# Mixture of experts on one core: weights split 2048 columns at a time, tokens gathered and outputs added by indirect DMA

## The chip, the cores and the metric

One core of one Trainium2 chip. The metric is the device time of one execution in microseconds (us), the median of three runs. Engines: PE (TensorE) multiplies matrices, DVE (VectorE) and ACT (ScalarE) work elementwise, POOL (GpSimd) and SP (SyncE) issue DMAs here.

## The reference, cut to what matters

The reference runs two blocks of two layers each on 256 tokens of 1024 features. The second layer of the second block has a mixture of experts in place of a feed-forward layer, and the change is there:

```python
def moe_swiglu(x2d, w_router, w_gate, w_up, w_down):
    ...
    top_logits, top_e = lax.top_k(logits, TOP_K)
    top_w = jax.nn.softmax(top_logits, axis=-1).reshape(-1)
    ...
    def expert_block(args):
        xb, e = args
        return (jax.nn.silu(xb @ w_gate[e]) * (xb @ w_up[e])) @ w_down[e]
    ...
    y = jax.ops.segment_sum(y_rows[dest] * w_sorted[:, None], tok_sorted, num_segments=n_tok)
```

There are 8 experts with an inner width of 3584, each token goes to two of them, and all is float32.

## The kernel before

Every product is made from float32 operands that are split into two parts of the type fp32r: a high half `h`, which ACT casts (line 368), and a low half `l`, which DVE makes as value minus `h` (line 369). `mm3` (lines 381 to 385) then adds three matmuls into one PSUM bank: high by high, high by low, low by high.

`moe` (line 1976) computes the norm `u` of the tokens, the router's logits and, for each token and expert, a weight, whether it is chosen, and its place among the expert's tokens. An expert has 128 places. Then it goes through the experts in order, and `expert` (line 2115) does the work of one.

- *Gather.* `gather` (line 2098) builds `D`, 0 or 1 for token by place, on DVE (line 2103), and multiplies `u` by it on PE (line 2111): 16 matmuls in float32 that give the expert's tokens, features on partitions. ACT and DVE split them to `xh` and `xl`. The gather of the next expert is called by `ahead()` in `expert`, after the last gate and up block.
- *Weights.* An expert's weights are 42 pieces of 128 x 2048, 1 MiB each: for each of 14 column blocks `ck`, two pieces for gate and up and one for down. `arrive` (line 349) fetches them by SP's queue into a ring of `NM` = 8 tiles `wv`. `parts` (line 358) splits 1024 columns at a time into tiles `wh` and `wl`; they come in turn from two rings of three pairs, so six pairs are there.
- *A block.* `up(ck)` multiplies the tokens by both gate and up pieces (24 matmuls of 512 columns into one bank); between the two it calls `turned(ck - 1)`, which transposes the block before (line 2129) and splits it to `me_hh` and `me_hl`. After it ACT takes the silu (line 2156) and DVE multiplies (line 2157). `down(ck - 1)` then adds 12 matmuls into the two banks `y`.
- *Back to the tokens.* At its end (lines 2169 to 2189) an expert transposes `D`, puts the weights in order of places (line 2173), scales and splits `y` to `me_yh` and `me_yl`, multiplies by the turned `D` (8 matmuls of 512 columns, lines 2187 and 2188), and DVE adds the result to the tokens `x` (four additions, line 2189).

After the eight experts a loop handles experts with more than 128 tokens; it runs as often as there are such experts.

The kernel is written as a sequence; the framework orders the instructions of each engine when the program is built, each as soon as its estimate has operands and a buffer ready, earlier ones first. On the chip each engine keeps that order, and semaphores hold it where an operand is not there. So PE may take matmuls of the next expert between those that end the last one, as the rows below show.

Of the kernel before, what the change touches and what calls it, by code (L numbers as in the profile page):

```python
# [11 lines left out]
F32 = mybir.dt.float32  # L12
F32R = mybir.dt.float32r
BF16 = mybir.dt.bfloat16
I32 = mybir.dt.int32
# [6 lines left out]
PIECE = 2048  # L22
# [67 lines left out]
def constants():  # L90
    t = Table()
    i = np.arange(128)
    r, c = i[:, None], i[None, :]
    t.add("ident", (r == c) * 1.0)
    t.add("causal", np.where(c > r, NEG, 0.0))
    d = i % 64
    t.add("freq", np.where(d < 8, -FREQ[d % 8], np.where(d < 16, FREQ[d % 8], 0.0)))
    d = i % 32
    t.add("freq_i", np.where(d < 4, -FREQ_I[d % 4], np.where(d < 8, FREQ_I[d % 4], 0.0)))
    t.add("freq_2", np.broadcast_to(FREQ_2, (128, 16)))  # L100

# [24 lines left out]
    t.add("eye64", (e == x[:, None]) * 1.0)  # L126
    t.add("g_strict", np.where(e < x[:, None], 0.0, NEG))
    t.add("g_incl", np.where(e >= x[:, None], 0.0, NEG))
    t.add("first", np.broadcast_to(np.where(np.arange(256) % 64 == 0, 0.0, 1.0), (128, 256)))
    t.add("before", (r < c) * 1.0)  # L130
    t.add("slot", np.broadcast_to(c, (128, 128)) * 1.0)
    f = np.arange(8)
    t.add("lower_e", np.broadcast_to((f[None, :] < f[:, None]) * 1.0, (128, 8, 8)))
    return t
# [118 lines left out]
ROUND = 12582912.0  # L253
NV, NH, NL = 3, 3, 3
NM = 8
PRE = ['31111111111111111', '11311131101111113']
COUNTS = ['111111121222211223022', '111111121322211222120']
ORDER = ['gmggmggmgmgmgmgggmggmggmggmggmggm', 'gmgggmgmgmgmggmgmgmggggmggmggmggm']
# [2 lines left out]
class Core:  # L261
# [96 lines left out]
    def parts(self, v, ring=None):  # L358
        n = v.shape[1]
        pool, _, nh, nl = ring or next(self.rings)  # L360
        h = pool.tile([128, HALF], F32R, tag="wh", name=self.name("wh"), bufs=nh)[:, :n]
        l = pool.tile([128, HALF], F32R, tag="wl", name=self.name("wl"), bufs=nl)[:, :n]
        self.split(h, l, v)
        return h, l

    def split(self, h, l, v):

# [1594 lines left out]
    def moe_first(self, pool):  # L1962

        rt = self.load(pool, "router", [128, 64])
        rh, rl = (self.sb(pool, [128, 8, 8], F32R) for _ in range(2))
        self.split(rh, rl, rt.rearrange("p (k e) -> p k e", k=8))
        return rh, rl, {n: self.cst(pool, n) for n in ("before", "slot", "lower_e")}

    def moe_ahead(self, ctx):

        self.big_ring(ctx, NM, 3, 3, side="right")
        self.moe_gain = self.row(self.arriving[0], "norm_ffn1")
        for j in (0, 1, 3, 4, 2, 6, 7, 5)[:NM]:
            self.early.append(self.arrive(self.A["moe"][j], True))

    def moe(self, rh, rl, c):
        nc, A = self.nc, self.A
        mm = nc.tensor.matmul
        with ExitStack() as ctx:
            pool = self.pool(ctx, "moe")  # L1980
            self.banks(mm=4, acc=4)

            x = self.feature_major(self.x, self.vec("norm_ffn1"))
# [1 line left out]
            p = self.psum()[:8, :256]  # L1985
            for k in range(8):
                self.mm3(p, (rh[:, k], rl[:, k]), (x[0][:, k], x[1][:, k]), k == 0, k == 7)
            lT = self.sb(pool, [8, 256])
            nc.vector.tensor_copy(lT, p)
            rc = self.norm_col(pool, z)  # L1990
            for n in range(4):
                for tt in range(2):
                    h = slice(n * 256, n * 256 + 256)
                    nc.scalar.activation(u[:, tt, h], self.x[:, tt, h], AF.Copy, scale=rc[tt])
                    nc.gpsimd.tensor_mul(u[:, tt, h], u[:, tt, h], self.moe_gain[:, h])
            ones = self.sb(pool, [128, 128])
            nc.gpsimd.memset(ones, 1.0)
            lg = self.sb(pool, [128, 2, 8])
            p = self.psum()[:, :16].rearrange("p (t e) -> p t e", t=2)
            for tt in range(2):  # L2000
# [77 lines left out]
            self.halves = itertools.cycle((0, 1))  # L2078
            chosen = lambda e: [[info[:, tt, j, e:e + 1] for j in range(3)] for tt in range(2)]
            ready = self.gather(pool, c, u, chosen(0))  # L2080
            for e in range(8):

                following = []
                ahead = (lambda: following.append(self.gather(pool, c, u, chosen(e + 1)))) if e < 7 else lambda: None
                self.expert(pool, ready, lambda i: moe[e, i], ahead, None if e else rest)
                ready = following[0] if following else None

            n = nc.values_load(count, min_val=0, max_val=3)
            with self.tc.For_i(0, n) as s:  # L2089
                lt = self.sb(pool, [128, 8], F32, "lt")  # L2090
                nc.sync.dma_start(lt, spill[bass.ds(s, 1)].rearrange("s p e -> (s p) e"))
                le = self.sb(pool, [1, 1], I32, "le")
                nc.vector.tensor_copy(le, lt[:1, 6:7])
                e = nc.sync.value_load(le, min_val=0, max_val=7)
                ready = self.gather(pool, c, u, [[lt[:, 3 * tt + j:3 * tt + j + 1] for j in range(3)] for tt in range(2)])
                self.expert(pool, ready, lambda i: moe[bass.ds(e, 1), i].rearrange("e p c -> (e p) c"), lambda: None)

    def gather(self, pool, c, u, info):

        nc = self.nc  # L2100
        D = self.sb(pool, [128, 2, 128], F32, "me_D", 2)
        for tt in range(2):
            last = nc.vector.tensor_scalar(D[:, tt], c["slot"], info[tt][2], info[tt][1], op0=ALU.is_equal, op1=ALU.mult)
# [11 lines left out]
    def expert(self, pool, ready, w, ahead, first=None):  # L2115


        nc = self.nc
# [14 lines left out]
            hs[ck] = hh, hl  # L2133

        def down(ck):
            d = self.arrive(w(3 * ck + 2))
            d = [self.parts(d[:, j * HALF:j * HALF + HALF]) for j in range(2)]
            hh, hl = hs.pop(ck)
            for j in range(2):
                for n in range(2):  # L2140
                    s = slice(n * 512, n * 512 + 512)
                    self.mm3(y[n], (hh[:, j], hl[:, j]), [t[:, s] for t in d[j]], ck == 0 and j == 0, ck == 13 and j == 1)

        def up(ck):
            p = self.psum()
            for i in range(2):
                v = self.arrive(w(3 * ck + i))
                for j in range(2):
                    h, l = [t.rearrange("p (k c) -> p k c", k=2) for t in self.parts(v[:, j * HALF:j * HALF + HALF])]
                    for k in range(2):  # L2150
                        kk = 4 * i + 2 * j + k
                        self.mm3(p, (xh[:, kk], xl[:, kk]), (h[:, k], l[:, k]), kk == 0, kk == 7)
                if i == 0 and ck:
                    turned(ck - 1)
# [4 lines left out]
        for ck in range(14):  # L2159
# [3 lines left out]
                first()  # L2163
            if ck:
                down(ck - 1)
        turned(13)
        ahead()
        down(13)
        p = self.psum()[:, :384]
        for tt in range(2):  # L2170
            nc.tensor.transpose(p[:, tt * 128:tt * 128 + 128], D[:, tt], self.ident)
        for tt in range(2):
            mm(p[:, 256:257], D[:, tt], weight[tt], start=tt == 0, stop=tt == 1)
        Dt = self.sb(pool, [128, 256], F32R, "me_Dt", 1)
        nc.scalar.copy(Dt, p[:, :256])
        wr = self.sb(pool, [128, 1], F32, "me_w", 2)
        nc.vector.tensor_copy(wr, p[:, 256:257])
        yh = self.sb(pool, [128, 1024], F32R, "me_yh", 1)
        yl = self.sb(pool, [128, 1024], F32R, "me_yl", 1)
# [60 lines left out]
```

## Time and profile before

| | |
|---|---|
| median of three runs | 3272.34 us (3271.23 to 3272.56) |
| the profiled execution, its own time | 3261.19 us |
| its span, first to last instruction | 3259.4 us |
| busy, share of the span | PE 96%, DVE 74%, ACT 57%, POOL 1% |
| experts, about | 2195 to 3220 us of the span |
| DMA, whole span | 691.10 MB, mean 212 GB/s |

PE is the matmul, PEld its weight load, which overlaps. Times in rows are in us from the span's start unless they are marked ns. A row of a timeline merges several like instructions (x4) and gives the time from the first's start to the last's end; in brackets stands how long the engine had been idle and what released it. Ends of matmuls are modelled (a matmul of 512 columns shows 0.39 us and the next one starts 0.23 later), so the starts tell the pace. A float32 matmul shows as two records; a transpose shows as one.

### The profile page before, as it was taken

How to read it: one execution, taken by the hardware profiler on the slowest of the kernel's cores; microseconds unless marked ns; L12 is line 12 of the kernel's file. 1: busy time of each engine (PE TensorE's matmuls, PEld its weight loads, DVE VectorE, ACT ScalarE, POOL GpSimd, SP SyncE). 2: the span in 40 equal slices, each digit the busy share in tenths (PEclk: the TensorE clock that was granted, in tenths of full speed). 3: DMA queues.
4: the chain of work that ended last, by engine and by line, in shares of the span. 5: the costliest groups of instructions: out<-in, count | busy, mean ns of one | idle time of the engine just before them, and what ended most of it. 6: DMA issues, size and time to landing. Idle time of an engine off the chain costs nothing. (4 is left out here: it accounts for less than half of the span.)

```text
span 3259.4 us, 52984 instructions
## 1 busy us (share of the span) xinstructions
PE 3135.3 (96%) x20906; PEld 2712.3 (83%) x20906; DVE 2399.8 (74%) x4079; ACT 1846.6 (57%) x2810; POOL 45.1 (1%) x87
## 2 busy tenths in 40 slices
PE   8998999999999899999998999989999999999998
PEld 8987699999779888888997888878887777777876
DVE  6567765656865686866557858569888888888886
ACT  5455544444454455544445445448777777777775
POOL 0000000000000000000001000000000000000000
PEclk9998999999999999999999999999999999999999
DMA  8434373551365143337733423479999898898994
GB/s 310 160 93 130 97 297 143 210 188 53 108 237 197 51 142 94 104 111 249 273 112 120 124 79 119 125 271 367 342 341 337 332 365 333 327 366 332 351 339 153
DMA packets 158159, 691.10 MB, mean 212 GB/s; under 512 B 41056, under 2 KB 55200, under 8 KB 94928
## 3 DMA queue, kind: packets, MB, share of 16 engines
q1 hardware_dynamic: 153984, 673.38, 57.2%
q0 software_dynamic: 3632, 14.03, 1.4%
q8 instruction: 166, 2.72, 0.3%
q14 instruction: 89, 0.73, 0.1%
q10 hardware_dynamic: 288, 0.23, 0.0%
HBM read 673.94 MB, written 13.64 MB: 211 GB/s over the span
## 5 line engine op out<-in xcount | busy, mean ns | idle before, releaser
L369 DVE TENSOR_TENSOR wl<-wv,wh 128x1024 fp32r<-128x1024 f32 x1256 | 1493.2, 1215 | 428.9 <-ACT wh L368 404.9
L368 ACT CAST wh<-wv 128x1024 fp32r<-128x1024 f32 x1256 | 1272.5, 1043 | 678.0 <-PE bank L384 356.0
L383 PE MATMUL bank<-xh,wh 128*128 128x256 f32 x2880 | 836.4, 290 | 19.1 <-ACT gt L1837 5.1
L384 PE MATMUL bank<-xl,wh 128*128 128x256 f32 x2880 | 825.9, 287 | 2.7 <-DVE r_i L448 1.8
L385 PE MATMUL bank<-xh,wl 128*128 128x256 f32 x2880 | 824.1, 286 | 1.6 <-DVE wl L369 1.6
L383 PEld LDWEIGHTS bank<-xh,wh 128*128 128x128 f32 x2880 | 555.4, 193 | 40.7 <-issue 11.8
L384 PEld LDWEIGHTS bank<-xl,wh 128*128 128x128 f32 x2880 | 555.8, 193 | 13.0 <-issue 2.8
L385 PEld LDWEIGHTS bank<-xh,wl 128*128 128x128 f32 x2880 | 555.0, 193 | 5.9 <-DVE wl L369 2.7
L384 PE MATMUL bank<-wl,xh 128*128 128x512 f32 x896 | 364.6, 407 | 5.9 <-DVE wl L369 5.9
L383 PE MATMUL bank<-wh,xh 128*128 128x512 f32 x896 | 357.3, 399 | 0.0
L385 PE MATMUL bank<-wh,xl 128*128 128x512 f32 x896 | 352.9, 394 | 0.0
L384 PEld LDWEIGHTS bank<-wl,xh 128*128 128x128 f32 x896 | 168.3, 188 | 56.2 <-DVE wl L369 24.2
L383 PEld LDWEIGHTS bank<-wh,xh 128*128 128x128 f32 x896 | 168.3, 188 | 37.0
L385 PEld LDWEIGHTS bank<-wh,xl 128*128 128x128 f32 x896 | 168.6, 188 | 34.3
L384 PE MATMUL bank<-wl,me_hh 128*128 128x512 f32 x448 | 177.7, 397 | 0.0
L385 PE MATMUL bank<-wh,me_hl 128*128 128x512 f32 x448 | 176.7, 395 | 0.0
L419 PE MATMUL bank<-wh,hh 128*128 128x512 f32 x440 | 172.8, 393 | 1.4 <-ACT hh L368 1.4
L420 PE MATMUL bank<-wl,hh 128*128 128x512 f32 x440 | 172.7, 393 | 0.0
L383 PE MATMUL bank<-wh,me_hh 128*128 128x512 f32 x448 | 157.5, 395 | 0.5 <-ACT me_hh L375 0.5
L422 PE MATMUL bank<-wh,hl 128*128 128x512 f32 x440 | 140.2, 393 | 0.0
L368 ACT CAST hh<-h 128x256 fp32r<-128x256 f32 x110 | 44.7, 406 | 136.5 <-DVE h L582 136.5
L375 ACT CAST me_hh<-bank 128x256 fp32r<-128x256 f32 x112 | 41.8, 373 | 117.4 <-PE bank L2129 117.4
(639 smaller groups left out, 4091.3 us busy)
## 6 DMA issues: line engine op xcount, KB each, us to landing
wv<-in_moe_dram SPq DMA_DIRECT2D x336, 1024.0 KB, 6.0
wv<-in_ffn_dram SPq DMA_DIRECT2D x120, 1024.0 KB, 5.1
wv<-in_ffn_d_dram SPq DMA_DIRECT2D x30, 1024.0 KB, 5.0
wv<-in_in_t_dram SPq DMA_DIRECT2D x48, 512.0 KB, 3.7
wv<-in_in_g_dram SPq DMA_DIRECT2D x34, 512.0 KB, 3.7
wv<-in_in_r_dram SPq DMA_DIRECT2D x28, 512.0 KB, 4.1
wv<-in_ffn_dram SPq DMA_DIRECT2D x24, 512.0 KB, 4.3
wv<-in_br_dram SPq DMA_DIRECT2D x24, 512.0 KB, 3.9
```

Source lines behind the costliest of these rows:

```text
L368: self.nc.scalar.copy(h, v)
L369: self.nc.vector.tensor_sub(l, v, h)
L375: nc.scalar.copy(h, p)
L383: mm(out, l[0], r[0], start=start, stop=False)
L384: mm(out, l[0], r[1], start=False, stop=False)
L385: mm(out, l[1], r[0], start=False, stop=stop)
L419: mm(p, x[0][:, s], w[0][:, c:c + n], start=first and r == 0, stop=False)
L420: mm(p, x[0][:, s], w[1][:, c:c + n], start=False, stop=False)
L422: mm(p, x[1][:, s], w[0][:, c:c + n], start=False, stop=last and r == len(rows) - 1)
```

## The change

- `wide` casts and subtracts all 2048 columns of a piece in one instruction each, into three pairs of tiles `ww` and `wx`. It is used for the second piece of gate and up and for the piece of down; the first piece stays in two halves, with the three pairs of the ring that remains.
- The tokens' norms `u` are written to `rows` in HBM, and the tokens `x` to `sums`, with 128 rows more to which empty places go. For experts 1 to 7 the tokens are fetched from `rows` by an indirect DMA of POOL's queue, called after block 3 of the expert before, and turned by 8 transposes where the gather stood. `targets` gets the row numbers from `D` with two small matmuls and four instructions of DVE.
- For experts 0 to 6 the scaled outputs are added to `sums` by an indirect DMA that accumulates. `x` is fetched back after block 3 of expert 7, whose own outputs are added as before.
- Some tiles share storage (`me_y`, `xn`, `me_g`), and the ones of the router come from the table of constants instead of a memset.

```diff
+    t.add("token", np.stack([i, i * 0 + 1, i + 128, i * 0 + 1, i + 256, -i - 256], 1) * 1.0)
...
+NW = 3
...
+    def wide(self, v):
+
+        h, l = (self.broad.tile([128, PIECE], F32R, tag=t, name=self.name(t), bufs=NW) for t in ("ww", "wx"))
+        self.split(h, l, v)
+        return [[t[:, j * HALF:j * HALF + HALF] for t in (h, l)] for j in range(2)]
...
-        self.big_ring(ctx, NM, 3, 3, side="right")
+        self.big_ring(ctx, NM, side="right")
...
-            ones = self.sb(pool, [128, 128])
-            nc.gpsimd.memset(ones, 1.0)
+            ones = c["token"][:, 1:2].to_broadcast([128, 128])
...
             ready = self.gather(pool, c, u, chosen(0))
+            rows, sums = (self.tc.dram_tile([n, 1024], F32, name=self.name("rows")) for n in (256, 384))
+            nc.gpsimd.dma_start(rows.rearrange("(t p) d -> p t d", p=128), u)
+            nc.gpsimd.dma_start(sums[:256].rearrange("(t p) d -> p t d", p=128), self.x)
+            nc.gpsimd.dma_start(sums[256:], u[:, 0])
             for e in range(8):
-                following = []
-                ahead = (lambda: following.append(self.gather(pool, c, u, chosen(e + 1)))) if e < 7 else lambda: None
-                self.expert(pool, ready, lambda i: moe[e, i], ahead, None if e else rest)
+                nxt, following = [], []
+                def send():
+                    if e < 7:
+                        nxt.append(self.places(pool, c, chosen(e + 1), rows))
+                    else:
+                        nc.gpsimd.dma_start(self.x, sums[:256].rearrange("(t p) d -> p t d", p=128))
+                def ahead():
+                    if e < 7:
+                        following.append(self.turn_in(*nxt[0]))
+                if e == 0:
+                    to = self.targets(pool, c, ready[0])
+                else:
+                    to = ready[5]
+                self.expert(pool, ready[:5], lambda i: moe[e, i], ahead, None if e else rest, send, (sums, to) if e < 7 else None)
                 ready = following[0] if following else None
...
+    def targets(self, pool, c, D):
...
+        tok = c["token"]
+        p = self.psum()[:, :2]
+        for tt in range(2):
+            nc.tensor.matmul(p, D[:, tt], tok[:, 2 * tt:2 * tt + 2], start=tt == 0, stop=tt == 1)
+        t = self.sb(pool, [128, 2], F32, "me_t", 2)
+        nc.vector.tensor_copy(t, p)
+        i = self.sb(pool, [128, 2], I32, "me_i", 3)
+        nc.vector.tensor_copy(i[:, 0:1], t[:, 0:1])
+        nc.vector.scalar_tensor_tensor(t[:, 1:2], t[:, 1:2], tok[:, 5:6], t[:, 0:1], op0=ALU.mult, op1=ALU.add)
+        nc.vector.tensor_scalar(i[:, 1:2], t[:, 1:2], tok[:, 4:5], None, op0=ALU.add)
+        return i
...
+    def places(self, pool, c, info, rows):
+
+        D, last = self.placed(pool, c, info)
+        to = self.targets(pool, c, D)
+        G = self.sb(pool, [128, 2, 1024], F32, "xn")[:, 0]
+        self.nc.gpsimd.indirect_dma_start(G, None, rows, bass.IndirectOffsetOnAxis(ap=to[:, 0:1], axis=0))
+        return G, D, [i[0] for i in info], last, to
+
+    def turn_in(self, G, D, weight, last, to):
...
+        for j in range(2):
+            p = self.psum().rearrange("p (k r) -> p k r", k=4)
+            for k in range(4):
+                f = (4 * j + k) * 128
+                self.nc.tensor.transpose(p[:, k], G[:, f:f + 128], self.ident)
+            self.split_p(xh[:, 4 * j:4 * j + 4], xl[:, 4 * j:4 * j + 4], p)
...
         def down(ck):
-            d = self.arrive(w(3 * ck + 2))
-            d = [self.parts(d[:, j * HALF:j * HALF + HALF]) for j in range(2)]
+            d = self.wide(self.arrive(w(3 * ck + 2)))
...
                 v = self.arrive(w(3 * ck + i))
+                parts = self.wide(v) if i else [self.parts(v[:, j * HALF:j * HALF + HALF]) for j in range(2)]
                 for j in range(2):
-                    h, l = [t.rearrange("p (k c) -> p k c", k=2) for t in self.parts(v[:, j * HALF:j * HALF + HALF])]
+                    h, l = [t.rearrange("p (k c) -> p k c", k=2) for t in parts[j]]
...
             if ck:
                 down(ck - 1)
+            if ck == 3:
+                send()
         turned(13)
         ahead()
         down(13)
...
+        if out:
+            ys = self.sb(pool, [128, 1024], F32, "me_y", 1)
+            for n in range(2):
+                nc.scalar.activation(ys[:, n * 512:n * 512 + 512], y[n], AF.Copy, scale=wr)
+            nc.gpsimd.indirect_dma_start(out[0], bass.IndirectOffsetOnAxis(ap=out[1][:, 1:2], axis=0), ys, None,
+                                         compute_op=ALU.add)
+            return
```

`gather` keeps its matmuls for expert 0 and takes `D` from a new helper `placed` (the two lines that built it). The loop for experts over 128 tokens uses `places` and `turn_in` too.

## Rows read from the trace of the kernel before

**Rows 1.** Windows: busy us by engine (instructions), granted clock, DMA share and GB/s

```profile
core 0: us, PE busy (x) PEld busy (x) DVE busy (x) ACT busy (x) POOL busy (x), PEclk, DMA share, GB/s
2195.00:3202.00 1007.00, 1000.87 (x4542) 803.77 (x4543) 893.70 (x1000) 733.46 (x915) 0.00 (x0) 1.00 0.91 342
2610.00:2620.00 10.00, 10.00 (x46) 8.08 (x45) 8.91 (x10) 7.61 (x10) 0.00 (x0) 1.00 0.96 378
40.00:50.00 10.00, 10.00 (x75) 9.51 (x74) 8.83 (x30) 5.53 (x10) 0.00 (x0) 1.00 1.01 420
```

**Rows 2.** Waits of PE and its weight loads in the stage: us, times, longest

```profile
PE bank L384 <- DVE wl L369: 5.9, 6, 1.0
...
PEld bank L384 <- DVE wl L369: 24.0, 55, 1.5
```

**Rows 3.** Timeline of PE, one steady period: start us, us, instruction

```profile
2649.26 0.38 PE L2129 MATMUL bank<-t,me_g 128*128 128x128 f32 x2
...
2652.04 0.39 PE L383 MATMUL bank<-wh,xh 128*128 128x512 f32 x1
2652.31 0.50 PE L384 MATMUL bank<-wl,xh 128*128 128x512 f32 x1
...
2654.74 0.39 PE L385 MATMUL bank<-wh,xl 128*128 128x512 f32 x1
...
2657.98 0.38 PE L2129 MATMUL bank<-t,me_g 128*128 128x128 f32 x2
```

**Rows 4.** Timeline of ACT in that period

```profile
2649.68 0.38 ACT L375 CAST me_hh<-bank 128x256 fp32r<-128x256 f32 x1 [0.95 <-PE bank L2129]
2649.95 3.89 ACT L368 CAST wh<-wv 128x1024 fp32r<-128x1024 f32 x4
2655.17 0.39 ACT L2156 ACTIVATE me_g<-bank 128x256 f32<-128x256 f32 x1 [1.33 <-PE bank L385]
2655.45 1.99 ACT L368 CAST wh<-wv 128x1024 fp32r<-128x1024 f32 x2
```

**Rows 5.** Timeline of DVE in that period

```profile
2651.03 4.63 DVE L369 TENSOR_TENSOR wl<-wv,wh 128x1024 fp32r<-128x1024 f32 x4 [0.52 <-ACT wh L368]
```

**Rows 6.** Timeline of PE at the end of expert 3, and of 6 (last)

```profile
2703.02 0.38 PE L2129 MATMUL bank<-t,me_g 128*128 128x128 f32 x2
2703.24 1.95 PE L2111 MATMUL bank<-me_D,xn 128*128 128x128 f32 x16
2704.94 0.48 PE L383 MATMUL bank<-wh,me_hh 128*128 128x512 f32 x1
...
2707.93 0.50 PE L2173 MATMUL bank<-t,me_D 128*128 128x1 f32 x4
...
2715.81 0.40 PE L383 MATMUL bank<-wh,xh 128*128 128x512 f32 x1
2717.24 0.50 PE L384 MATMUL bank<-wl,xh 128*128 128x512 f32 x1 [1.03 <-DVE wl L369]
...
3093.54 0.50 PE L2173 MATMUL bank<-t,me_D 128*128 128x1 f32 x4
```

**Rows 7.** Timeline of DVE at the same place

```profile
2711.33 1.40 DVE L379 SCALAR_TENSOR_TENSOR me_yl<-bank,me_w,me_yh 128x512 fp32r<-128x512 f32 x2
2713.46 2.59 DVE L2189 TENSOR_TENSOR x<-bank,x 128x512 f32<-128x512 f32 x4 [0.73 <-PE bank L2188]
```

**Rows 8.** Groups by shape, ACT and DVE: busy us, mean ns, idle before

```profile
L368 ACT CAST wh<-wv 128x1024 fp32r<-128x1024 f32 x1228 | 1250.8, 1049 | 645.7 <-PE bank L384 340.8 <-issue 173.6 <-PE bank L422 42.9
...
L368 ACT CAST hh<-h 128x256 fp32r<-128x256 f32 x110 | 44.7, 406 | 136.5 <-DVE h L582 136.5
...
L369 DVE TENSOR_TENSOR wl<-wv,wh 128x1024 fp32r<-128x1024 f32 x1228 | 1468.4, 1222 | 422.6 <-ACT wh L368 398.6 <-DMA wv<-in_ffn_d_dram 8.7 <-DMA wv<-in_ffn_dram 7.0
...
L369 DVE TENSOR_TENSOR hl<-h,hh 128x256 fp32r<-128x256 f32 x110 | 46.7, 425 | 48.1 <-ACT hh L368 48.1
```

**Rows 9.** DMA issues: count, KB each, median us from issue to landing

```profile
x<-kept POOLq DMA_DIRECT2D x2, 1024.0 KB, 6.6
```

More of the change, by code (lines that the diff above doesn't have):

```diff
@@ L1966, in moe_first @@
         self.split(rh, rl, rt.rearrange("p (k e) -> p k e", k=8))
-        return rh, rl, {n: self.cst(pool, n) for n in ("before", "slot", "lower_e")}
+        return rh, rl, {n: self.cst(pool, n) for n in ("before", "token", "slot", "lower_e")}
     def moe_ahead(self, ctx):
-        self.big_ring(ctx, NM, 3, 3, side="right")
+        self.big_ring(ctx, NM, side="right")
         self.moe_gain = self.row(self.arriving[0], "norm_ffn1")
@@ L1979, in moe @@
         with ExitStack() as ctx:
-            pool = self.pool(ctx, "moe")
+            pool = self.broad = self.pool(ctx, "moe")
             self.banks(mm=4, acc=4)
@@ L1987, in moe @@
                 self.mm3(p, (rh[:, k], rl[:, k]), (x[0][:, k], x[1][:, k]), k == 0, k == 7)
-            lT = self.sb(pool, [8, 256])
+            lT = self.sb(pool, [8, 256], F32, "me_g", 3)
             nc.vector.tensor_copy(lT, p)
@@ L2094, in moe @@
                 e = nc.sync.value_load(le, min_val=0, max_val=7)
-                ready = self.gather(pool, c, u, [[lt[:, 3 * tt + j:3 * tt + j + 1] for j in range(3)] for tt in range(2)])
+                info = [[lt[:, 3 * tt + j:3 * tt + j + 1] for j in range(3)] for tt in range(2)]
+                ready = self.turn_in(*self.places(pool, c, info, rows))[:5]
                 self.expert(pool, ready, lambda i: moe[bass.ds(e, 1), i].rearrange("e p c -> (e p) c"), lambda: None)
+    def targets(self, pool, c, D):
+        nc = self.nc
+        tok = c["token"]
[9 more added lines that the diff above has]
+        return i
@@ new lines, in placed @@
+    def placed(self, pool, c, info):
+        D = self.sb(pool, [128, 2, 128], F32, "me_D", 2)
+        for tt in range(2):
+            last = self.nc.vector.tensor_scalar(D[:, tt], c["slot"], info[tt][2], info[tt][1], op0=ALU.is_equal, op1=ALU.mult)
+        return D, last
+    def places(self, pool, c, info, rows):
[4 more added lines that the diff above has]
+        return G, D, [i[0] for i in info], last, to
@@ new lines, in turn_in @@
+    def turn_in(self, G, D, weight, last, to):
+        half = slice(next(self.halves) * 128, None)
+        xh, xl = (t[:, :, half][:, :, :128] for t in (self.xh, self.xl))
+        for j in range(2):
[4 more added lines that the diff above has]
+            self.split_p(xh[:, 4 * j:4 * j + 4], xl[:, 4 * j:4 * j + 4], p)
+        return D, xh, xl, weight, last, to
@@ L2098, in gather @@
     def gather(self, pool, c, u, info):
         nc = self.nc
-        D = self.sb(pool, [128, 2, 128], F32, "me_D", 2)
-        for tt in range(2):
-            last = nc.vector.tensor_scalar(D[:, tt], c["slot"], info[tt][2], info[tt][1], op0=ALU.is_equal, op1=ALU.mult)
+        D, last = self.placed(pool, c, info)
         half = slice(next(self.halves) * 128, None)
@@ L2113, in gather, with expert @@
         return D, xh, xl, [i[0] for i in info], last
-    def expert(self, pool, ready, w, ahead, first=None):
+    def expert(self, pool, ready, w, ahead, first=None, send=lambda: None, out=None):
         nc = self.nc
@@ L2170, in expert @@
         for tt in range(2):
+            mm(p[:, 256:257], D[:, tt], weight[tt], start=tt == 0, stop=tt == 1)
+        wr = self.sb(pool, [128, 1], F32, "me_w", 2)
+        nc.vector.tensor_copy(wr, p[:, 256:257])
+        if out:
[5 more added lines that the diff above has]
+            return
+        for tt in range(2):
             nc.tensor.transpose(p[:, tt * 128:tt * 128 + 128], D[:, tt], self.ident)
-        for tt in range(2):
-            mm(p[:, 256:257], D[:, tt], weight[tt], start=tt == 0, stop=tt == 1)
         Dt = self.sb(pool, [128, 256], F32R, "me_Dt", 1)
         nc.scalar.copy(Dt, p[:, :256])
[L2176 to L2179, printed above, removed]
+        yh, yl = self.sb(pool, [128, 1024], F32R, "me_y", 1), self.sb(pool, [128, 1024], F32R, "xn")
         for n in range(2):
```

## The prediction

> **What bounds the kernel now.** I read the windows first, then the waits, then the timelines of one steady period and of one change of expert. In the windows the expert stage is 1007 us of the 3259.4 us span, with PE busy for 1000.87, DVE for 893.70, ACT for 733.46, and PE's granted clock at 1.00, its 2.4 GHz level [rows 1]. A busy PE is not yet PE at its peak, since the ends of matmuls are modelled, so the waits come next: in the whole stage PE itself waits only for `wl`, the low half of a weight that DVE makes, 5.9 us in 6 waits, and its weight loads 24.0 us in 55 [rows 2]. No DMA is in that list. So PE's own work sets the stage, and DVE stands close behind it.
>
> The timeline shows the unit. One period (one `ck`: a gate/up column block and a down block, 36 matmuls of 512 columns and two transposes) runs from 2649.26 to 2657.98, 8.72 us [rows 3]. From 2654.74 to 2657.98 there are 14 matmul starts, so one costs 0.231 us; 36 of them are 8.33, and two transposes at 0.11 (2703.02 to 2703.24 for two [rows 6]) make it 8.55. The missing 0.17 us sits at the second weight piece of the period: the first matmul on the high half starts at 2652.04, and the next, on the low half, later than a pitch would have it [rows 3]. ACT and DVE show why. ACT waits 0.95 us for the transposes, casts `me_hh`, and only then, at 2649.95, begins the four casts of the second and third piece [rows 4]; DVE subtracts behind it from 2651.03 [rows 5] and has the first low half 1.22 us later [rows 8], at 2652.25. So the chain transposes, `me_hh`, cast, subtraction, PE is just in time. There are 112 such periods (14 for each of 8 experts).
>
> The change of expert is dearer. The second half of the gather takes 1.70 us of PE (16 records, two for each of its 8 matmuls, 2703.24 to 2704.94); the first half's 16 are strewn between earlier matmuls. Then come the transposes of `D`, the little weight product, and 8 matmuls of 512 columns that add the outputs to the tokens. And PE stands still from 2715.81 to 2717.24 [rows 6], since DVE, which should make `wl`, is doing `me_yl` (1.40) and four additions to `x` (2.59) instead [rows 7]. From one change of expert to the next it is (3093.54 - 2707.93) / 3 = 128.5 us [rows 6].
>
> **The change, part by part.**
>
> *Gather.* For experts 1 to 7 the 32 records (2 x 1.70 = 3.40 us) give way to 8 transposes at 0.11, 0.88: 2.52 us less on PE, 17.6 for seven. Taking the first half at the second's price is a choice; were those records only filling gaps, half of this would be lost. The splits of `xh` and `xl` stay. The gather by DMA is issued after `ck` 3 and read after `ck` 13, under some ten periods, 87 us. No row has an indirect DMA; the nearest is a copy of 1 MB by the same queue, 6.6 us to landing [rows 9], for twice the bytes. Even five times that is hidden. If that cover is gone, PE waits at `turn_in`.
>
> *Adding to rows outside.* For experts 0 to 6 the eight matmuls (8 x 0.231 = 1.85) and two transposes (0.22) go: 2.07 us, 14.5 for seven. DVE loses the 1.40 and the 2.59 [rows 7], so the standstill behind them should go, 5.9 us over six [rows 2]. What is late next is the ordinary 0.17 of a period. ACT's two scalings of `y` stay. The accumulating DMA has until the next expert's `ys`, some 120 us, and the last one until `x` is fetched back, after `ck` 3 of expert 7. That load has ten periods before the last additions. On POOL's queue gather, accumulation and the fetch of `x` wait for each other, but nothing else stands behind them in this stage, and SP's queue, which carries the weights, gets no instruction more.
>
> *New small work.* `targets` makes two matmuls of two columns, four records, each like the little weight product (0.50 us for four [rows 6]): 7 x 0.50 = 3.5 us on PE. Its four DVE instructions and the two that build `D` are no dearer than today's, which are only moved to `ck` 3; DVE pays for them from the 3.99 it saves. The three writes before the loop (2.6 MB) run beside weights, of which eight pieces are fetched ahead. If that doesn't cover them, they cost at the stage's best rate, 378 GB/s [rows 1], 6.9 us once; I take 0.
>
> *Weights 2048 columns at a time.* This is the term that decides. Two of the three pieces of a period are cast and subtracted in one instruction each. From the rows of 256 and 1024 columns ACT takes (1049 - 406) / 768 = 0.84 ns a column and DVE (1222 - 425) / 768 = 1.04 [rows 8]; so a wide cast is 1049 + 857 = 1.91 us and a wide subtraction 1222 + 1063 = 2.28. Four casts in a row take 3.89 and four subtractions 4.63 [rows 4, 5], so two wide ones in place of four narrow save next to nothing, and on engines that PE rarely waits for. But the low half comes only when all 2048 columns are through. Bound below: the wide pieces are made a block earlier, as three wide pairs and three narrow hold nine halves where six are held now, and the 0.17 of each period goes: 112 x 0.17 = 19 us gained. Bound above: ACT's order stays as it is [rows 4]. Then the cast ends at 2649.95 + 1.91 = 2651.86, the subtraction at 2654.14, and PE gets its low half 1.89 us later than the 2652.25 of today: 112 x 1.89 = 212 us lost. I take zero, near the lower end. ACT stands idle for 0.95 and 1.33 us in each period [rows 4] and DVE for 0.52 before its four subtractions [rows 5]. That is room to run ahead, and with a third wide buffer free, what keeps the cast behind `me_hh` is only the order of issue.
>
> *The sum:* 17.6 + 14.5 + 5.9 - 3.5 = 34.5 us less. The profiled execution took 3261.19 us, 1.8 more than its span and 0.3% under the median of 3272.34; I take the same 34.5 from the median: 3237.8, say 3238.
>
> **A rule that speaks against it.** Weights of one expert are 42 pieces of 1 MiB, 44.0 MB; gather and accumulation (a read and a write) add 1.6. At 128.5 - 5.1 = 123.4 us an expert that asks for 370 GB/s. The stage moves 342 on average, 378 in a window of 10 us inside it, and 420 was reached early in the kernel [rows 1], so I count transfers as hidden. The Trainium skill, "DMA: Bandwidth & Descriptors", section Specifications, gives about 358 GB/s as the limit of a core on HBM. By that an expert could not take less than 127.4 us, an estimate from the page, and the kernel would stand near 3265. The trace has gone past that figure in both windows, and the measurement decides; but ten microseconds don't prove a thousand.
>
> **The rivals.**
> - *Transfers become the bound.* The mechanism: the ring of eight pieces empties, and PE waits for `wv`. The price by rows: a period moves 3 MiB in 8.72 us, 361 GB/s, the most that was held for long. With 45.6 MB that is 126.4 us an expert, 2.1 less than now, so 7 x 2.1 = 15 us and 3257. For it: 0.91 of the DMA time is taken already. Against it: not one wait on a DMA. Chance 0.19.
> - *The wide split comes late (slower).* Place: the second piece of each period, by the chain above. Price: up to 1.89 us in 112 periods, 212 us, less the 34.5: about 3450. It decides once the low half comes 34.5 / 112 = 0.31 us later than today in every period. For it: the chain is just in time, and PE takes the low half as the second of three matmuls [rows 3], with ten more behind it. Against it: the idle time of ACT and the third pair. Chance 0.24; in 0.05 of it the loss about cancels the gain.
> - *The change doesn't relieve PE as said:* the gather's records fill gaps, and only their second half counts. 7 x 1.26 = 9 us less gain: 3247. This lies within my range and goes with the forecast.
>
> **How the numbers follow.** The forecast's mechanism has 0.57, all faster. Of the transfers' 0.19, 0.12 is still faster and 0.07 the same. Of the late split's 0.24, 0.05 is the same and 0.19 slower. That gives faster 0.69, same 0.12, slower 0.19; 0.2%, 6.5 us, is about what a measurement of this kernel can tell from no change. The low end is the forecast less the 19 us of the periods and some for smaller errors, 3215. The high end takes in transfers, no gain at all, and a split that is late by 0.46 us in each period: 3238 + 112 x 0.46 = 3290. Beyond it lies the rest of the late split, some 0.13. The forecast's own range, without the rivals, is 3215 to 3250.
>
> **What would show it.** In the profile after: 8 transposes by `turn_in` where 32 records of the gather stood; the scatter's matmuls and `x` additions in the last expert alone; a change of expert every 122 to 124 us; the steady period still between 8.55 and 8.72 us; the stage's rate up by some 25 GB/s. I am wrong if the period grows, with PE waiting for `wl` between a matmul on the high half and the next; if PE waits for a DMA of `wv`, or of the gathered rows; or if ACT or DVE shows a wait for the pairs of 2048 columns.

## The result, and the profile after

| | before | after |
|---|---|---|
| median, runs side by side | 3272.45 us (3271.23 to 3275.95, 4 runs) | 3228.52 us (3227.26 to 3239.44, 4 runs) |
| the profiled execution, its span | 3261.19, 3259.4 | 3239.44, 3237.7 |
| expert stage, first silu to last | 1006.0 | 967.4 |
| one expert, steady (by the weight product) | 128.5 | 122.35 |

The ratio is 0.9873, with a 95% interval from 0.9854 to 0.9891: 36 to 48 us less. The predicted 3238 was 9.5 us too high; the range held it. Before's profiled execution lay 11 us under its median and after's 11 us over: the code ahead of the experts, which the change hardly touches, took 17 us longer in the second (first `D` at 2212.1 us, before at 2194.7), at a mean granted clock over the span of 0.978 against 0.984. The stage itself has a granted clock of 1.00 in both, so the terms are settled on it: 38.6 us less. The medians lie 5.3 us further apart than that; this part is not in the stage, and no trace shows where it comes from. The stage's length is in the view of one source line, the silu of each kernel (count, duration in ns, first and last start). Before:

```profile
L2156 ACT ACTIVATE me_g<-bank x112: 384/384/388, 2207.4 to 3213.4; 128x256 f32<-128x256 f32 x112
```

After:

```profile
L2223 ACT ACTIVATE me_g<-bank x112: 383/385/387, 2224.8 to 3192.2; 128x256 f32<-128x256 f32 x112
```

The window over the stage of after answers to [rows 1] (same columns):

```profile
2225.00:3192.00 967.00, 964.85 (x4320) 779.24 (x4319) 848.62 (x755) 708.34 (x690) 48.20 (x15) 1.00 0.95 363
```

PE is still the bound, with 2.15 us not busy in 967. In a window 40 us shorter DVE is busy 45 us less and ACT 25. The transfers rose from 342 to 363 GB/s at 0.95 of the DMA time. The waits of PE and its weight loads in the stage, all of them, against [rows 2]:

```profile
PEld bank L393 <- DVE me_hl L384: 3.8, 7, 2.4
PE bank L393 <- DVE me_hl L384: 2.0, 1, 2.0
PEld bank L392 <- DVE wx L377: 1.6, 5, 0.3
PEld bank L391 <- ACT me_hh L383: 1.6, 6, 0.3
PEld bank L2195 <- DVE me_g L2224: 0.4, 1, 0.4
```

The waits for the low half `wl`, 5.9 and 24.0 us before, are gone; for its wide form `wx` 1.6 us are left. No DMA is in the list. One steady period on PE, against [rows 3]:

```profile
2656.75 0.38 PE L2195 MATMUL bank<-t,me_g 128*128 128x128 f32 x2
2656.89 0.47 PE L391 MATMUL bank<-ww,xh 128*128 128x512 f32 x1
2657.20 0.39 PE L392 MATMUL bank<-wx,xh 128*128 128x512 f32 x1
...
2665.34 0.38 PE L2195 MATMUL bank<-t,me_g 128*128 128x128 f32 x2
```

8.59 us where it was 8.72. ACT in that period, against [rows 4]:

```profile
2654.40 1.90 ACT L376 CAST ww<-wv 128x2048 fp32r<-128x2048 f32 x1
2657.17 0.37 ACT L383 CAST me_hh<-bank 128x256 fp32r<-128x256 f32 x1 [0.86 <-PE bank L2195]
2657.43 1.06 ACT L376 CAST wh<-wv 128x1024 fp32r<-128x1024 f32 x1
2659.96 0.39 ACT L2223 ACTIVATE me_g<-bank 128x256 f32<-128x256 f32 x1 [1.47 <-PE bank L393]
2660.24 1.04 ACT L376 CAST wh<-wv 128x1024 fp32r<-128x1024 f32 x1
2661.18 3.71 ACT L376 CAST ww<-wv 128x2048 fp32r<-128x2048 f32 x2
2665.75 0.37 ACT L383 CAST me_hh<-bank 128x256 fp32r<-128x256 f32 x1 [0.86 <-PE bank L2195]
```

The order is another one. Before, `me_hh` came first and the casts of the second and third piece behind it; now both wide casts stand ahead of `me_hh`. DVE, against [rows 5], follows them and has the first `wx` through at about 2656.8, 0.4 us before PE wants it:

```profile
2654.54 4.50 DVE L377 TENSOR_TENSOR wx<-wv,ww 128x2048 fp32r<-128x2048 f32 x2
2658.95 0.42 DVE L384 TENSOR_TENSOR me_hl<-bank,me_hh 128x256 fp32r<-128x256 f32 x1
```

PE at the end of expert 3 and of expert 6 (last), against [rows 6]:

```profile
2699.68 0.38 PE L2195 MATMUL bank<-t,me_g 128*128 128x128 f32 x2
...
2700.14 0.60 PE L2162 MATMUL bank<-t,xn 128*128 128x128 f32 x4
...
2705.95 0.50 PE L2240 MATMUL bank<-t,me_D 128*128 128x1 f32 x4
...
2706.57 0.60 PE L2162 MATMUL bank<-t,xn 128*128 128x128 f32 x4
...
3073.01 0.50 PE L2240 MATMUL bank<-t,me_D 128*128 128x1 f32 x4
```

Eight transposes stand where the gather's records were, and neither a matmul that adds outputs nor a standstill follows: (3073.01 - 2705.95) / 3 = 122.35 us an expert. Groups by shape, against [rows 8]:

```profile
L377 DVE TENSOR_TENSOR wx<-wv,ww 128x2048 fp32r<-128x2048 f32 x222 | 501.7, 2289 | 22.8 <-ACT ww L376 18.8
L376 ACT CAST ww<-wv 128x2048 fp32r<-128x2048 f32 x221 | 412.7, 1906 | 5.7 <-PE bank L393 5.7
...
L2247 POOL DMA_INDIRECT rows<-me_y,me_i x7 | 30.1, 4295 | 643.2 <-ACT me_y L2246 643.2
L2152 POOL DMA_INDIRECT xn<-rows,me_i x7 | 17.3, 2478 | 176.5 <-issue 135.6 <-PE bank L2195 40.9
```

The DMA issues in the stage, against [rows 9]:

```profile
wv<-in_moe_dram SPq DMA_DIRECT2D x325, 1024.0 KB, 7.0
x<-rows POOLq DMA_DIRECT2D x1, 1024.0 KB, 11.9
xn<-rows,me_i POOLq DMA_INDIRECT x7, 10.0
rows<-me_y,me_i POOLq DMA_INDIRECT x7, 14.6
```

### The profile page after: what moved, and what is told of

The parts are those of the page before. It is cut to its first block, busy times and chain, and to the rows that moved or that the text cites. A ratio compares the mean times of both kernels' runs of the same rounds, so it can differ in the third digit from the quotient of the medians.

```text
span 3237.7 us, 51923 instructions
## 1 busy us (share of the span) xinstructions
PE 3118.9 (96%) x20700; PEld 2703.8 (84%) x20700; DVE 2353.9 (73%) x3845; ACT 1817.9 (56%) x2579; POOL 95.4 (3%) x105
## 5 line engine op out<-in xcount | busy, mean ns | idle before, releaser
L377 DVE TENSOR_TENSOR wl<-wv,wh 128x1024 fp32r<-128x1024 f32 (+1 forms) x808 | 969.6, 1210 | 355.6 <-ACT wh L376 337.8
L376 ACT CAST wh<-wv 128x1024 fp32r<-128x1024 f32 (+1 forms) x808 | 836.1, 1039 | 670.5 <-PE bank L392 363.6
L377 DVE TENSOR_TENSOR wx<-wv,ww 128x2048 fp32r<-128x2048 f32 x224 | 506.2, 2289 | 22.8 <-ACT ww L376 18.8
L376 ACT CAST ww<-wv 128x2048 fp32r<-128x2048 f32 x224 | 418.3, 1906 | 5.7 <-PE bank L393 5.7
L391 PE MATMUL bank<-ww,xh 128*128 128x512 f32 x448 | 185.3, 414 | 0.0
L392 PE MATMUL bank<-wx,xh 128*128 128x512 f32 x448 | 177.9, 397 | 0.0
L393 PE MATMUL bank<-ww,xl 128*128 128x512 f32 x448 | 177.5, 396 | 0.0
L391 PE MATMUL bank<-wh,xh 128*128 128x512 f32 x448 | 176.4, 394 | 0.0
L392 PE MATMUL bank<-wl,xh 128*128 128x512 f32 x448 | 175.8, 392 | 0.0
L393 PE MATMUL bank<-wh,xl 128*128 128x512 f32 x448 | 175.1, 391 | 0.0
```

Of the source, the lines that this page charges most:

```text
L376: self.nc.scalar.copy(h, v)
L377: self.nc.vector.tensor_sub(l, v, h)
L391: mm(out, l[0], r[0], start=start, stop=False)
L392: mm(out, l[0], r[1], start=False, stop=False)
L393: mm(out, l[1], r[0], start=False, stop=stop)
```

## The experiments

The kernel before was run again beside each group of kernels, with medians from 3263.7 to 3273.2 us, so a whole time compares only with the before of its group: 3263.72 for held, nw2, allwide and traffic6, 3267.54 for each3. Outside the stage the traces differ as well, from 2253 to 2274 us, in code that the edits hardly touch; a ratio is therefore coarser than a stage. The distance between experts repeats within 0.1 us (held aside), and most verdicts rest on it: from the last silu of one expert to the last of the next, experts 2 to 6 (they are counted from 0). The table gives it, the steady period, and the stage from the first silu to the last.

| kernel | stage | an expert | period | time, or ratio to before |
|---|---|---|---|---|
| before | 1006.0 | 128.5 | 8.72 | |
| after | 967.4 | 122.37 | 8.59 | 0.9873 |
| narrow: after with 1024 columns | 974.9 | 123.94 | 8.74 | 0.9932 [0.9915, 0.9948] |
| gather_mm: after, gather on PE | 981.5 | 124.63 | 8.59 | 0.9945 [0.9925, 0.9965] |
| scatter_mm: after, adding on PE | 984.1 | 124.85 | 8.59 | 0.9934 [0.9912, 0.9955] |
| wide_only: before with 2048 columns | 989.0 | 125.95 | 8.55 | 0.9957 [0.9941, 0.9974] |
| held: after, wide casts behind `me_hh` | 1153.4 | about 146 | 10.0 | 3418.64 (one run) |
| nw2: two wide pairs | 968.0 | 122.7 | 8.59 | 3243.54 (one run) |
| allwide: first piece wide too | 992.9 | 124.46 | 8.62 | 3256.72 (one run) |
| traffic6: copies, all at once | 1061.0 | see text | 8.59 | 3329.65 (one run) |
| narrow6: narrow, nine halves | 976.9 | 124.17 | 8.76 | 0.991 [0.9896, 0.9925] |
| each3: copies tied to each gather | 967.5 | 122.40 | 8.59 | 3243.2 (one run) |
| ahead6: narrow6, casts ahead of `me_hh` | 967.6 | 122.85 | 8.59 | 0.9908 [0.9889, 0.9926] |

**Which part gives what.** Four kernels take one part back, or make one alone.

```diff
 narrow:
+        return [self.parts(v[:, j * HALF:j * HALF + HALF]) for j in range(2)]
-        h, l = (self.broad.tile([128, PIECE], F32R, ...) for t in ("ww", "wx"))
...
-        self.big_ring(ctx, NM, side="right")
+        self.big_ring(ctx, NM, 3, 3, side="right")
```

> The changed kernel, but every piece is split 1024 columns at a time again, from two rings of three pairs. Theory (the wide split runs ahead and takes the 0.13 us of waiting out of each of some 112 periods): the steady period goes back from 8.585 to about 8.72 us and the time to about 3228.5 + 15 = 3243 us, 29 less than before. Rival (the wide split is worth nothing, the whole gain is PE's work at the change of expert): 3228 to 3231 us with the period unchanged. If the change of expert needs the wide split to get rid of its standstill, 3249.

```diff
 gather_mm:
-                        nxt.append(self.places(pool, c, chosen(e + 1), rows))
+                        pass
...
-                        following.append(self.turn_in(*nxt[0]))
+                        r = self.gather(pool, c, u, chosen(e + 1))
+                        following.append(r + (self.targets(pool, c, r[0]),))
```

> The changed kernel, but experts 1 to 7 get their tokens by the 16 float32 matmuls again (the row numbers for the accumulating DMA are still made). Theory (PE pays for each of the 32 records): 7 x 2.52 = 17.6 us more, 3246 us. Rival (the first half only filled gaps): 9 us more, 3237 us. Rival (gather was hidden altogether): 3229.

```diff
 scatter_mm:
...
-                self.expert(..., send, (sums, to) if e < 7 else None)
+                self.expert(..., send)
```

The edit also leaves out what fills `sums` and fetches `x` back from it.

> The changed kernel, but all experts add their outputs by matmuls and by DVE again; tokens still come by the indirect DMA. Theory (PE pays 2.07 us and DVE's 3.99 us make PE stand still for 0.8 to 1 us): 14.5 + 5.9 us more, 3249 us, with a wait of PE for a low half at each change of expert. Rival (the wide split runs far enough ahead to cover DVE's additions): 14.5 us more, 3243 us, and no such wait.

wide_only is the kernel before with `wide` and its three pairs; gather and addition are made on PE as before, the outputs in two halves of 512 columns.

> The kernel before with the wide split alone; gather and scatter by matmuls (the outputs are added in halves of 512 features, one pair of tiles in turn, as there is no room for two pairs). Theory: 112 periods shorter by 0.13 us, 15 us less than before, 3257 us; if the wide split also covers the standstill at the change of expert, 21 us less, 3251. Rival (the wide split alone is worth nothing or comes late): 3272 us or more.

An expert takes 1.57 us longer without the wide split, 2.26 without the gather by DMA, and 2.48 without the addition by DMA. From the other side, the wide split alone takes 2.55 off the kernel before, and both DMAs together take 3.58 off wide_only (125.95 to 122.37). This is less than 2.26 + 2.48, because each of gather_mm and scatter_mm still pays for `targets`, which the other DMA needs: 0.44 us, by the period where it stands in after (9.03 for 8.59). Another part of the gap is that the period of these kernels is 8.59 and that of wide_only 8.55: the matmuls of `wx` by `xh`, on the second piece, start 0.233 us apart in after and 0.228 in wide_only, while those of `wx` by `me_hh`, on the piece of down, have 0.235 and 0.236. Over an expert all its 512-column matmuls take 118.65 us in after and 118.13 in wide_only. Why is not settled, and 0.2 us of the gap are left.

**The order on ACT.** held asks for another order alone: the wide cast of the second piece may be issued on ACT only behind the cast of `me_hh`. (The framework then orders PE's matmuls anew, too.)

```diff
+            hs["cast"] = nc.scalar.copy(hh.rearrange("p j r -> p (j r)"), p)
...
-                parts = self.wide(v) if i else [...]
+                with self.tc.issue_after(hs["cast"].ins) if i and ck else nullcontext():
+                    parts = self.wide(v) if i else [...]
```

> The changed kernel with one thing more: ACT's wide cast of the second piece is put behind the cast of me_hh in ACT's order, where the first narrow cast stood before the change (an order of issue only, no wait is added). Theory (the wide split gains only because ACT's order moved it a block ahead): the low half comes at least 1.9 us late in every period, PE waits for it there, the steady period goes from 8.59 to 10.5 us or more, an expert from 122.4 to about 149, the kernel to some 3430 us. Rival (the third pair and the idle time of ACT and DVE make the place in the order unimportant): the period stays below 8.75.

The timeline of ACT in this run, and then, from its waits, the lines on `ww`:

```profile
2702.68 0.37 ACT L2198 CAST me_hh<-bank 128x256 fp32r<-128x256 f32 x1 [2.17 <-PE bank L2195]
2702.95 3.71 ACT L376 CAST ww<-wv 128x2048 fp32r<-128x2048 f32 x2
2706.55 2.00 ACT L376 CAST wh<-wv 128x1024 fp32r<-128x1024 f32 x2
2710.10 0.39 ACT L2225 ACTIVATE me_g<-bank 128x256 f32<-128x256 f32 x1 [1.54 <-PE bank L393]
2712.66 0.37 ACT L2198 CAST me_hh<-bank 128x256 fp32r<-128x256 f32 x1 [2.18 <-PE bank L2195]
```

```profile
PEld bank L391 <- ACT ww L376: 113.1, 116, 2.5
PE bank L391 <- ACT ww L376: 77.8, 69, 2.3
```

The period is 10.0 us, 1.28 more than before where I had bounded the loss at 1.89, and the kernel takes 155 us more than the before of its group. The rival of the late split was a real one. The profile names a wait for `ww` and not for the low half, because PE's order now has two matmuls on the piece of down between the second piece's high and low half; but the low half is late as feared:

```profile
2704.89 4.49 DVE L377 TENSOR_TENSOR wx<-wv,ww 128x2048 fp32r<-128x2048 f32 x2 [1.38 <-ACT ww L376]
2706.70 0.73 PE L391 MATMUL bank<-ww,me_hh 128*128 128x512 f32 x2 [1.06 <-ACT ww L376]
2707.28 0.46 PE L392 MATMUL bank<-wx,xh 128*128 128x512 f32 x1
```

The first of the two subtractions, 2.29 us long, is through at 2707.18, and PE takes its `wx` at 2707.28. The stage is 186 us longer than that of after. Of this the period alone makes 112 x 1.40 = 157 us. The rest can't be told apart from the clock, which was granted at 0.97 over this stage and at 1.00 over that of after:

```profile
2219.00:3372.00 1153.00, 1031.57 (x4325) 783.84 (x4324) 860.58 (x753) 716.68 (x693) 18.85 (x15) 0.97 0.79 304
```

narrow6 and ahead6 ask whether the width, the room or the order makes the gain. narrow6 has the room of after, nine halves, and splits 1024 columns at a time; ahead6 puts the second piece's two narrow casts ahead of `me_hh`.

```diff
 narrow6, on after:
+        return [self.parts(v[:, j * HALF:j * HALF + HALF], (self.broad, NM, 2 * NW, 2 * NW)) for j in range(2)]
 ahead6, on narrow6:
+                    parts = second
...
+                if i == 0:
+                    second = self.wide(self.arrive(w(3 * ck + 1)))
                 if i == 0 and ck:
                     turned(ck - 1)
...
+            with self.tc.issue_after(self.cast.ins):
+                nc.scalar.copy(hh.rearrange("p j r -> p (j r)"), p)
```

> The changed kernel with the same space as its three wide pairs, but split 1024 columns at a time: the second and the down piece take their halves from a ring of six `wh` and six `wl`, the first piece keeps its three, so nine halves are held and only the width of the instruction differs from the kernel after. Theory A, what counts is the room: with nine halves the casts of the second piece can be ordered a block ahead, before `me_hh`, and the width of 2048 columns is worth nothing. Then the steady period is 8.59 us, the distance between experts 122.4, and the kernel takes about 3228, as the kernel after does. Theory B, what counts is the width (fewer, longer instructions with less to start and fewer handshakes): then it stays as in the run with narrow splits and six halves, period 8.74, 123.9 an expert, about 3250. If an instruction of half the width gives its low half earlier and this mattered, it would be a little under 122.4, down to 8.55 x 14 + 2.2 = 121.9.

> The run with nine narrow halves, with ACT's order alone changed: the two casts of the second piece are issued ahead of the one of `me_hh`, as in the kernel after, where that run has them behind it (period 8.76, 124.17 us an expert). Everything is still split 1024 columns at a time. Theory A, the order is the whole of the wide split's gain: the period falls to 8.55 to 8.59 us, an expert to 121.9 to 122.4, PE's weight loads wait for `wl` next to nothing (22.5 us in 66 before), and the kernel takes 3225 to 3230. Theory B, the length of the instruction is the gain (two wide subtractions take 4.50 us where four narrow ones take 4.63, a little more slack in each period): it stays at 8.7 to 8.76 and 123.9 to 124.2, about 3239 to 3250. If the early casts make `me_hh` late instead, PE waits for `me_hh` or `me_hl` and an expert is longer than 124.2.

With the room alone nothing is gained; ACT's timeline in narrow6 has the old order, `me_hh` and then four casts:

```profile
2655.95 0.38 ACT L381 CAST me_hh<-bank 128x256 fp32r<-128x256 f32 x1 [0.99 <-PE bank L2193]
2656.22 3.89 ACT L374 CAST wh<-wv 128x1024 fp32r<-128x1024 f32 x4
```

and in ahead6 the four narrow casts stand ahead, and `me_hh` waits for nothing but them:

```profile
2660.52 3.89 ACT L374 CAST wh<-wv 128x1024 fp32r<-128x1024 f32 x4
2664.30 0.37 ACT L2197 CAST me_hh<-bank 128x256 fp32r<-128x256 f32 x1
```

The waits for `wl` in a window of 780 us of narrow6, and then of ahead6:

```profile
PEld bank L390 <- DVE wl L375: 22.5, 66, 0.4
```

```profile
PEld bank L390 <- DVE wl L375: 5.8, 12, 0.6
```

Narrow instructions in the new order reach the period of after, 8.59. So in the period the order is the whole gain of the wide split, and the width is worth nothing by itself; in the kernel after that order came along with the wide pairs, without an edit that asks for it. Why the framework chose it there, and whether it could be had with the six halves of before, no run shows. Over the expert ahead6 is 0.48 us longer, at the change of expert, and gains as much once in experts 0 and 1: its stage is as long as that of after. Its ratio lies 0.0035 above that of after, and their intervals overlap. It is also only 0.0002 below that of narrow6, whose stage is 9.3 us longer: the whole times don't resolve this gain, and it rests on the stage in one trace of each.

nw2 sets `NW = 2`, and allwide splits the first piece wide too (`parts = self.wide(v)` for both).

> The changed kernel with two pairs for wide splits in place of three. Theory (it is the order on ACT that counts; a pair comes free 5.6 us before it is needed again, and cast and subtraction take 4.2): period 8.6 to 8.75 us, an expert 122.4 to 125, at most 18 us more. Rival (the third pair is what lets ACT run ahead): 9.5 us or more a period, an expert 135 or more, at least 90 us more in all.

> The changed kernel with the first piece of a block split 2048 columns at a time too, all from the same three pairs. If PE is the bound and the split has room, the period stays at 8.55 to 8.65 us and the time within 5 us of the changed kernel. If the first piece's low half is what comes just in time, PE waits for it once in a period, by up to 1.1 us (2.28 for a wide subtraction less 1.22 for a narrow one): 9.7 us, some 120 us more.

nw2 lost 0.3 us an expert: the third pair, on which I had leaned, is hardly needed. allwide lost 2.1 us an expert, most of it where the experts change, since PE there waits for `me_hl`, which now stands behind a wide subtraction on DVE: 9.2 us in 8 waits. It lost 13 us more in experts 0 and 1, so the 5 us that I had allowed it were far too few; why these two are worse is open.

**Room in the transfers.** traffic6 and each3 copy 1 MiB from HBM to HBM, six or three times in an expert.

```diff
 traffic6:
+            more = [self.tc.dram_tile([256, 1024], F32, name=self.name("more")) for _ in range(2)]
...
+            if more and ck in (4, 5, 7, 8, 10, 11):
+                nc.gpsimd.dma_start(more[1], more[0])
 each3:
+                        with self.tc.issue_after(nxt[0][5].ins):
+                            for _ in range(3):
+                                nc.gpsimd.dma_start(more[1], more[0])
```

> The changed kernel with six copies of 1 MiB from HBM to HBM more in each expert, by POOL's queue, after blocks 4, 5, 7, 8, 10 and 11 (they move nothing that is used). An expert then asks for 45.6 + 6.3 = 51.9 MB as the queues count it. Theory (transfers have headroom up to about the 420 GB/s seen early in the kernel, and not more): 51.9 MB at 420 GB/s are 123.6 us, so an expert takes 123 to 126 us, with first waits of PE or ACT for wv. Rival (the limit lies near what is moved now, 360 to 378 GB/s): 137 to 144 us an expert, at least 100 us more in all. Rival (copies cost the weights nothing): 122.4 and no wait.

> The changed kernel with three copies of 1 MiB from one place outside to another in each of the first seven experts, issued on POOL's queue behind that expert's gather, so that the gather itself is not queued behind them and they cannot all run at the start. They add 3.1 MB read and 3.1 MB written to the 45.6 MB of an expert. Theory A, the transfers still have room (windows of the run with six copies showed 416 to 430 GB/s with PE busy throughout): experts stay at 122.4 us and the kernel near 3228 to 3240, with windows behind the gather at 410 to 430 GB/s. Theory B, the stage is close to what the transfers can do and eight pieces ahead only cover short bursts: PE waits for `wv`, and an expert takes about (45.6 + 6.3) / 0.363 GB/us = 143 us, the kernel some 145 us more.

traffic6 did not run as it was meant. Every copy writes the same rows, and on POOL each waited for the one before to land. So they ran one after another from 2214 to 2574 us, and accumulations and gathers stood behind them in POOL's order; the gather of expert 2 was issued only at 2536, and PE waited 50.1 us for it. The weights came late too: ACT waited for `wv` in 44 waits, 76.5 us, and with 419 to 424 GB/s in each stretch of 40 us from 2260 to 2460 PE was no longer busy throughout. So while a copy was always under way, the transfers were a bound, at some 420 GB/s. Experts 0 and 1 together took 94 us longer than in after; the later ones, with the copies all but done, took 122.35. The waits of traffic6, and one of those stretches:

```profile
PE bank L2164 <- DMA xn<-rows,me_i: 50.1, 1, 50.1
ACT ww L376 <- DMA wv<-in_moe_dram: 44.1, 26, 4.9
ACT wh L376 <- DMA wv<-in_moe_dram: 32.4, 18, 4.9
```

```profile
2300.00:2340.00 40.00, 36.09 (x158) 28.18 (x157) 30.70 (x24) 24.48 (x23) 2.44 (x5) 1.00 1.00 419
```

each3 asked for less and lost nothing: experts at 122.40, the stage at 967.5, the list of PE's waits as in after; ACT waited for `wv` twice, 4.3 us. Its windows (a stretch in which two copies and then the weights catching up fill the DMA time, and the whole stage):

```profile
2390.00:2430.00 40.00, 40.00 (x177) 32.33 (x177) 33.85 (x28) 29.25 (x28) 0.99 (x2) 1.00 1.01 420
2225.00:3194.00 969.00, 966.85 (x4328) 781.02 (x4328) 850.57 (x761) 709.91 (x692) 59.55 (x36) 1.00 0.97 386
```

At 420 GB/s for 40 us, with all of the DMA time taken, PE is busy throughout; over the stage 386 GB/s cost nothing. (The 23 GB/s above after are the 21 copies of 1.05 MB, counted once.) A bound by transfers stood further off than the rival had it: near 420 GB/s, by traffic6, and not at 361.

## Why the prediction was right, and where it was off

**The bound.** Right: PE's own work sets the stage, and the gain is what came off PE and what it waited for. By PE's starts over one expert, `turn_in` takes 0.98 us where the gather took 3.3 (in gather_mm), and the eight matmuls that added the outputs took 1.86 (in scatter_mm).

**Gather.** Predicted 2.52 an expert; measured 2.26 (gather_mm). The choice to count both halves held: the strewn records of the first half did cost PE time, and the rival "the gather's records fill gaps", 1.26 an expert, falls. The indirect gather lands in 10.0 us, within the five times 6.6 that I had allowed, and some 85 us are there for it.

**Adding to rows outside.** Predicted 2.07 on PE, and 0.98 for the standstill; measured 2.48 (scatter_mm). The first part held: by PE's starts the matmuls take 1.86 and the transposes 0.22; the other 0.4 us are matmuls on the weights that start later in scatter_mm. But the standstill was put down to this edit alone. scatter_mm keeps DVE's `me_yl` and `x` additions, and with the new order on ACT PE itself waits for no low half of a weight there; narrow, with the old order and the addition by DMA, has no such wait of PE either. The standstill goes with either edit, so it can't be credited to both.

**New small work.** 0.50 an expert predicted, 0.44 measured. What the sum missed is the start: expert 0 is 1.8 us slower than before, and expert 1 begins with the one wait of PE for `me_hl`, 2.0 us, so that it gains 3.9 instead of 6.15. Little of this is the small work. narrow has the same `targets` and the same three writes, and there expert 0 is 0.5 us slower than before, and expert 1 takes 123.91, as long as the later ones. The other 1.3 and 2.3 us come with the wide split: at that wait, DVE makes `me_hl` only behind a wide subtraction (the kernel after):

```profile
2338.47 2.28 DVE L377 TENSOR_TENSOR wx<-wv,ww 128x2048 fp32r<-128x2048 f32 x1
2340.67 0.42 DVE L384 TENSOR_TENSOR me_hl<-bank,me_hh 128x256 fp32r<-128x256 f32 x1
```

**Weights 2048 columns at a time.** This is the term that was mis-sized. I took 0, "near the lower end". It gave 7.5 us of the stage on top of the two DMAs (974.9 to 967.4: seven times 1.57, less the 3.6 at the start) and 17.0 alone (1006.0 to 989.0). The durations were right, 1.91 and 2.28 predicted for 1.906 and 2.289. The reason given, that ACT's idle time and a free pair let the cast run ahead, with the order of issue the only obstacle, was right in its last clause: the order did change (ACT's timeline), and it is what decides (held, ahead6). More room alone gained nothing (narrow6), and two pairs in place of three lost next to nothing (nw2). The lower end of 19 us was also counted over too many periods: before, the first full periods of an expert took 8.57 us, and only seven of 14 the 8.72 that I read. So 0.17 x 7 x 8 = 9.5 us was to be had there, and with the 5.9 of the standstill 15.4, which is most of what wide_only gave.

**The sum.** By experts: 0 takes 1.8 more, 1 takes 3.9 less, 2 to 6 take 6.15 less each (30.8), 7 takes 5.7 less: 38.6. Predicted were 34.5, all of it for the two DMAs; those gave 31.1 (narrow), and the wide split the other 7.5. (Taken the other way round, the wide split gives 17.0 and the DMAs 21.6, as both remove the standstill.) So the terms of the DMAs were 3.4 us too large and the one that I had put at nothing 7.5 too small; that they partly cancel in the sum is luck.

**Transfers.** The rival did not come: no wait of PE on a DMA, at 363 GB/s for 967 us. For it I had weighed a limit of a core of about 358 GB/s. The Trainium skill, "HBM Reference", section Specifications (TRN2), says that this is the share of a core when both cores of a pair stream, and that a core alone measures about 425 GB/s. The trace agrees with that: 420 for 40 us in each3 without a wait of PE, and 419 to 424 in traffic6, where ACT waited for weights. The 358 that I weighed is not the limit of this kernel, which runs on one core.

**The wide split comes late.** It did not happen, but held shows that it was no small chance wrongly given: at the same edit, ACT's order decided between 39 us gained and 147 lost in the stage, part of the 147 at a lower clock. The forecast was safe from it only by an order that the framework chose and that I had not foreseen.

## What to carry to other kernels

Where one engine feeds another just in time, read the order of issue from the timeline before the width of an instruction: here the same instructions in another order made the stage 9 us shorter (ahead6 against narrow6) or 186 longer (held against after). When two edits each remove the same stall, measure each alone, since only one of them can be credited with it. And a queue that holds a gather needed at a fixed moment must not be given work that nothing paces.

## What was not expected of the hardware

- An indirect DMA of 512 KB keeps POOL for 2.5 us (gather) and 4.3 us (accumulate) by the profile, and lands after 10.0 and 14.6 us beside a stream of weights that goes on at 363 GB/s. A piece of weights takes 7.0 us instead of 6.0 to land, and nobody waits for it.
- With copies from HBM to HBM beside the weights, 420 GB/s by the profile's count went on for 40 us in each3 without a wait on PE. At 419 to 424 GB/s for 200 us, in traffic6, ACT waited for weights and PE stood idle at times.
- Matmuls of the same shape and names (`wx` by `xh`) start 0.228 us apart in wide_only and 0.233 in after. All of the matmuls together differ by some 0.5 us an expert, and the cause stays open.
